# The fourth gate's weights: the low half by a subtraction on the chip in place of an accumulating DMA

## The chip, the cores and the metric

One core of a Trainium2 chip runs the whole program. Its engines are TensorE (matmuls, called PE in the profile, with PEld for its weight loads), VectorE (DVE), ScalarE (ACT), GpSimd (POOL) and SyncE (SP), which here only issues DMAs. Each engine takes its instructions strictly in the order in which they were written, and starts one when the semaphores it waits for are set. The metric is device time in microseconds (us) for one call of the kernel, lower is better.

## The reference

One layer of a hybrid decoder for a prompt of 1024 tokens and 8 single-token samples, which share their weights. What is computed around the change:

```python
h = rmsnorm(x, g_mix)
u = h @ w_in                      # 1024 -> 1536 columns
a    = u[..., :512]               # pooling branch
val  = u[..., 512:1024]
gate = u[..., 1024:]
glu  = val * jax.nn.sigmoid(gate)
yb   = conv_mixer(g_ext, ...)     # causal depthwise conv, 31 taps, on glu
x = x + concat(ya, yb) @ w_out
x = x + cross_attn(rmsnorm(x), k, v) @ w_o
x = x + (silu(h @ w_gate) * (h @ w_up)) @ w_down
```

All arrays are float32, and the result must be of float32 accuracy.

## The kernel before

**Split operands.** The large matmuls of this kernel get their operands as `fp32r`, and for accuracy each operand is held as two such parts, high and low, and a product is made in three passes: high by high, low data by high weights, high data by low weights (`PASSES`). So each block of raw weights, 128 x 1024, has to be turned into a tile `w` of two parts before PE can use it. There are two ways:

- `split`: one pass copies the raw weights into the high part (ACT or POOL, L373 or L375), and one subtraction, raw minus high, makes the low part (DVE or POOL, L384).
- `split_by_dma`: one pass copies the raw weights into the high part (L395 on ACT or L397 on POOL), a second pass writes minus the high part into the low part (the same line), and a DMA issued by POOL (L402) adds the raw weights from HBM onto it (`accum_op=ADD`).

The table `BY_DMA` names, for each weight array, the blocks that go the second way.

```python
        if j in BY_DMA.get(name, ()):
            split_by_dma(lambda p: w[:, p], lambda p: (w, p), lambda: raw[:], 1024, [(raw,)],
                         lambda: io[name][j], [], name not in ("w_dn", "w_dn2"))
        else:
            split(lambda p: w[:, p], lambda p: (w, p), lambda: raw[:], 1024, [(raw,)])
```

**What runs where.** Blocks of `w_in` come in pairs gate, value for the four channel groups (blocks 0 to 7: the gates are 0, 2, 4, 6), then four blocks of the pooling branch. A block gives one group of 72 matmuls on PE, L480, eight steps over the 1024 inputs by three passes by three column chunks of 344 tokens. Behind PE, DVE multiplies the gate's PSUM result by the norm factor (L714), ACT takes the sigmoid (L715), POOL multiplies once more (L716), and DVE multiplies with the value's result into `glu` (L730). The blocks of the pooling branch leave PSUM by L836 on DVE, with a tiny copy of the last 8 columns, L806.

**The convolution** of the 512 channels in four groups fills DVE, ACT and POOL beside PE. Half of its taps are multiply-adds on DVE (L682, L684, accumulating in PSUM, `cacc`). The other half are products on ACT into one of four rotating buffers (L664, `cp`; sometimes POOL, L665) that are added to `y` by POOL or DVE (L667, one after the other, since all add to the same rows; the lengths 511 down to 497 tell which tap a row is). L654 starts such a chain, L692, L693, L696, L697 and L701 end a group, L703 adds its sum to the total.

**Behind it** the memory keys (L850; their PSUM is emptied by L854 on DVE, then split by L373 or L375 and L384 into `kT`), values (L927, L932), windows of the pooling branch (L814 to L828, on POOL or DVE) and its small map (L870) are put on PE before the output projection (L480, `oa`, `ob`), the queries and the scores, and then the feed-forward part (L1323), which takes half of the span.

**What sets the order.** The pieces are named in the table `ORDER` (`g3 v3` is the fourth gate and value). `Program.order` goes through all tasks with modelled costs, and decides at each step which task is written next and, where a task may run on two engines, on which one. A planner's cost therefore decides at build time who makes a tap or a split. Buffers are reused by tags; `w` has two places (so the weights of a group are made while PE works on the group before), `raw` has three. The weights of the fourth gate are block 6 of `w_in`; their tile is `w_871` in the rows below, their raw tile `raw_549`.

Of the kernel before, what the change touches and what calls it, by code (L numbers as in the profile page):

```python
# [46 lines left out]
)  # L47

BY_DMA = {"w_in": (3, 4, 6, 7, 9, 10, 11), "w_k": (2, 3, 5), "w_o": (4, 5, 6), "w_out_a": (1,), "w_out_b": (3,), "w_q": (4, 5, 6), "w_v": (0, 7), "w_dn": (18, 19), "w_dn2": (1,)}
WIDE = ("w_k", "w_v")  # L50
LEAD = {"w_k": 2, "w_v": 3, "w_out_a": 15, "w_q": 15, "w_in": 1, "w_out_b": 12, "w_o": 8}
LAST_SPANS = ((0, 512), (512, 260), (772, 260))
# [208 lines left out]
def hybrid_step_kernel(ctx: ExitStack, tc: tile.TileContext, io):  # L261
# [11 lines left out]
    def buf(name, tag, shape, dtype=F32):  # L273
        return Buf(name, tag, shape, dtype)
# [115 lines left out]
    def split_by_dma(dst, key, src, n, r, again, again_keys, pool_too=False):  # L390


        def scaled(e, p, src, factor):
            if e is nc.scalar:
                e.activation(dst(p), src, AF.Copy, scale=factor)  # L395
            else:
                e.tensor_scalar(dst(p), src, factor, 1.0, ALU.mult, ALU.mult)  # L397

        either = {"ACT": act(n), "Pool": pool_ts(n)} if pool_too else {"ACT": act(n)}
        add(either, lambda e: scaled(e, 0, src(), 1.0), r, [key(0)])  # L400
        add(either, lambda e: scaled(e, 1, f32(dst(0)), -1.0), [key(0)], [key(1)])
        add({"Pool": 0.6}, lambda e: e.dma_start(dst(1), again(), accum_op=ALU.add), [key(1)] + again_keys, [key(1)], nbytes=4 * P * n)  # L402
# [38 lines left out]
    def w_prep():  # L441
# [3 lines left out]
        w = buf(f"w{i}", "op" if name in WIDE or i >= len(seq) - 4 else "w", (P, 2, 1024), F32R)  # L445
        if j in BY_DMA.get(name, ()):
            split_by_dma(lambda p: w[:, p], lambda p: (w, p), lambda: raw[:], 1024, [(raw,)],
# [1399 lines left out]
```

## Time and profile before

| | us |
|---|---|
| median of 3 runs | 1219.01 |
| lowest and highest of them | 1218.43, 1219.83 |
| the profiled execution | 1218.82 |
| its span, first to last instruction | 1217.0 |
| PE busy in it | 1197.5 |
| DVE, ACT, POOL busy | 928.6, 526.1, 246.3 |
| 0 to 35 us | first loads, first gate and value |
| 35 to 148 us | remaining blocks of `w_in`, with the convolution on DVE, ACT and POOL |
| 148 to 215 us | memory keys and values, pooling windows and map, start of the output projection |
| 215 to 545 us | output projection, queries, attention |
| 545 to 1217 us | feed-forward part and final norm |

A row of the profile's groups or of its timeline has the source line, the engine, the operation and the tiles (out<-in, buffer numbers left out). In the timeline the first number is the start, the second how long the row lasted; a bracket gives the idle time of that engine just before, and what ended it. Consecutive instructions of one kind stand as one row with their number (x9).

### The profile page before, as it was taken

Reading aid. Unit: us, or ns where it says so; the run is one execution under the profiler, and the core shown is the slowest. Engines: PE = TensorE matmul, PEld = TensorE weight load, DVE = VectorE, ACT = ScalarE, POOL = GpSimd, SP = SyncE. Lnnn points to the kernel's source line nnn. Section 1 sums busy time; section 2 is a strip of 40 time slices with the busy share of each in tenths; the row PEclk is TensorE's granted clock in tenths of the full one; section 3 lists DMA queues with packets and bytes.
Section 4 is the critical chain, followed back from the end, with each engine's and each line's share of the span. In section 5 each row is a group of like instructions: output and inputs, shape, how many; then the busy total and the mean of one; then the engine's idle time right before and its main releaser. Section 6 shows DMA issues by size and latency. Waiting matters only on the chain.

```text
span 1217.0 us, 19404 instructions
## 1 busy us (share of the span) xinstructions
PE 1197.5 (98%) x7720; PEld 1122.1 (92%) x7720; DVE 928.6 (76%) x1551; ACT 526.1 (43%) x720; POOL 246.3 (20%) x294
## 2 busy tenths in 40 slices
PE   8999999999999999999999999999999999999997
PEld 7999988999999979989999999999999999999886
DVE  7999999766258875779777787777867797879754
ACT  7765656445134633444222322233222365544533
POOL 3568842231111102111000000000000034332101
PEclk9999999999999999999999999999999999999999
DMA  7335677326395773521332232222313598678612
GB/s 289 83 76 114 145 211 222 119 103 212 105 294 181 235 276 111 157 104 62 105 114 79 98 114 107 107 83 98 123 70 105 203 319 242 178 185 226 150 52 88
DMA packets 60586, 180.75 MB, mean 149 GB/s; under 512 B 7824, under 2 KB 11600, under 8 KB 59216
## 3 DMA queue, kind: packets, MB, share of 16 engines
q1 hardware_dynamic: 53824, 157.92, 37.6%
q0 software_dynamic: 6672, 21.60, 10.2%
q8 instruction: 60, 0.98, 0.3%
q14 instruction: 30, 0.25, 0.1%
HBM read 145.72 MB, written 33.78 MB: 147 GB/s over the span
## 4 chain that ended last, share of the span: by engine, by line
PE 80%; DVE 3%; DMA 1%; ACT 0%; issue 0%; DVEq 0%; ACTq 0%
PE pr L1323 49%; PE ps L480 7%; PE po L480 7%; PE fd L1666 6%; PE oa L480 4%; PE ob L480 4%; PE sc L1023 1%; PE vps L927 1%; DMA w<-in_w_q 1%; PE pv L1081 1%; PE kps L850 0%; PE pmap L870 0%; DVE spcache_k L1120 0%; DMA spcache_k<-in_cache_k 0%; DVE oo L1086 0%; DVE pT L1067 0%
## 5 line engine op out<-in xcount | busy, mean ns | idle before, releaser
L1323 PEld LDWEIGHTS pr<-ab,wTb 128*128 128x128 f32 x1056 | 132.1, 188 | 3.6
L1323 PE MATMUL pr<-ab,wTa 128*128 128x260 f32 x1056 | 133.6, 282 | 0.0
L1323 PE MATMUL pr<-ab,wTb 128*128 128x260 f32 x1056 | 133.3, 282 | 0.0
L1323 PEld LDWEIGHTS pr<-ab,wTa 128*128 128x128 f32 x1056 | 130.7, 189 | 2.0 <-DVE su L1339 0.3
L1323 PE MATMUL pr<-ab,wG 128*128 128x512 f32 x528 | 128.8, 393 | 0.0
L1339 DVE TENSOR_TENSOR su<-pr,su 128x520 f32<-128x520 f32 (+1 forms) x112 | 77.7, 695 | 57.4 <-PE pr L1323 57.2
L480 PE MATMUL ps<-xop,w 128*128 128x344 f32 x720 | 114.1, 320 | 0.0
L1323 PEld LDWEIGHTS pr<-ab,wG 128*128 128x128 f32 x528 | 96.3, 188 | 18.8
L480 PEld LDWEIGHTS ps<-xop,w 128*128 128x128 f32 x720 | 113.6, 188 | 0.0
L1323 PEld LDWEIGHTS pr<-hb,dV 128*128 128x128 f32 x768 | 98.7, 188 | 4.4 <-DVE pp L1339 0.3
L1323 PE MATMUL pr<-hb,dV 128*128 128x260 f32 x768 | 100.2, 283 | 0.0
L480 PE MATMUL ps<-xq,w 128*128 128x344 f32 x576 | 94.8, 321 | 0.4 <-DMA w<-in_w_q 0.4
L480 PEld LDWEIGHTS po<-oo,w 128*128 128x128 f32 x576 | 90.9, 188 | 0.6 <-DVE oo L1086 0.4
L480 PEld LDWEIGHTS ps<-xq,w 128*128 128x128 f32 x576 | 90.7, 188 | 0.8 <-DMA w<-in_w_q 0.7
L480 PE MATMUL po<-oo,w 128*128 128x344 f32 x576 | 91.4, 320 | 0.0
L684 DVE SCALAR_TENSOR_TENSOR cacc<-glu,vec,cacc 128x511 f32<-128x511 f32 (+14 forms) x116 | 76.9, 742 | 0.0
L1323 PE MATMUL pr<-hb,dW 128*128 128x512 f32 x288 | 74.4, 394 | 0.0
L373 ACT ACTIVATE w<-raw 128x1024 fp32r<-128x1024 f32 (+1 forms) x37 | 35.0, 951 | 81.7 <-issue 20.1
L1666 PE MATMUL fd<-ho,w 128*128 128x260 f32 (+1 forms) x432 | 69.0, 321 | 0.0
L1666 PEld LDWEIGHTS fd<-ho,w 128*128 128x128 f32 x432 | 62.0, 188 | 6.8 <-issue 0.5
L1350 POOL MEMSET su<- 128x16 f32 x22 | 2.5, 112 | 310.0 <-PE pr L1323 244.0
L1323 PE MATMUL pr<-ab,wU 128*128 128x512 f32 x264 | 64.8, 394 | 0.0
(306 smaller groups left out, 2183.7 us busy)
## 6 DMA issues: line engine op xcount, KB each, us to landing
gr<-in_w_gu SPq DMA_DIRECT2D x44, 512.0 KB, 3.6
hb<-su SPq DMA_DIRECT2D x8, 1040.0 KB, 4.6
hs<-hb SPq DMA_DIRECT2D x16, 520.0 KB, 6.3
dr<-in_w_dn SPq DMA_DIRECT2D x16, 512.0 KB, 3.7
spcache_k<-in_cache_k SPq DMA_DIRECT2D x12, 512.0 KB, 6.3
hs<-hb SPq DMA_DIRECT2D x12, 512.0 KB, 4.7
raw<-in_w_in SPq DMA_DIRECT2D x10, 512.0 KB, 3.8
hb<-he SPq DMA_DIRECT2D x8, 520.0 KB, 3.4
```

Source lines behind the costliest of these rows:

```text
L373: e.activation(dst(0), src(), AF.Copy, scale=1.0 if gain is None else gain)
L480: e.matmul(ps[:, c, :CW], w[:, wi, cols], x[:, xi, c * CW : (c + 1) * CW], start=first and p == 0, stop=last and p == 2)
L684: e.scalar_tensor_tensor(acc[h][:, n:], src[:, : HALF - n], w, acc[h][:, n:], ALU.mult, ALU.add)
L927: e.matmul(ps[:, m], memg[k // 4][:, xi, k % 4, m * P : (m + 1) * P], w[:, wi, col : col + 512], start=(k == 0 and p == 0), stop=(k == KT ...
L1023: e.matmul(bank()[:, i * NMEM : (i + 1) * NMEM], qop[2 * h + dt][:, qi, tt * P : (tt + 1) * P], kk[:, ki, 2 * (h % 2) + dt], start=(dt == ...
L1081: e.matmul(ps[:, c], v[:, vi, m, col : col + P], pT[h][m][:, pi, sl], start=(m == 0 and p == 0), stop=(m == 1 and p == 2))
L1323: e.matmul(bank(c), w[:, wi, cols(j)], xs[0](j, xi)[:, c * n : (c + 1) * n], start=onto is None and j == 0 and p == 0, stop=j == nj - 1 an ...
L1339: from_sums(sums, "DVE", dve, lambda e, src, sl: e.tensor_tensor(as_banks(o(sl), src), src, as_banks(a(sl), src), op), [akey], [okey])
L1350: add({"Pool": 0.12}, lambda e: e.memset(o(), 0.0), [], keys)
L1666: e.matmul(view(i), w[:, wi, col : col + P], hops[k][:, xi, half, lo - half * HALF + i * width // count : lo - half * HALF + (i + 1) * wid ...
```

## The change

The number 6 leaves the list of `w_in` in `BY_DMA`. The fourth gate's weights are then made by `split` and no longer by `split_by_dma`.

```diff
-BY_DMA = {"w_in": (3, 4, 6, 7, 9, 10, 11), "w_k": (2, 3, 5), "w_o": (4, 5, 6), "w_out_a": (1,), "w_out_b": (3,), "w_q": (4, 5, 6), "w_v": (0, 7), "w_dn": (18, 19), "w_dn2": (1,)}
+BY_DMA = {"w_in": (3, 4, 7, 9, 10, 11), "w_k": (2, 3, 5), "w_o": (4, 5, 6), "w_out_a": (1,), "w_out_b": (3,), "w_q": (4, 5, 6), "w_v": (0, 7), "w_dn": (18, 19), "w_dn2": (1,)}
```

The order of the instructions on PE and on SP is the same as before. On ACT, DVE and POOL the planner's order is different from the fourth gate's weights to the start of the output projection, and the same again from there.

On ACT, where the fourth gate's weights are made (`cacc_1_576` is the odd accumulator of the first convolution group, `w_981` and `w_983` the weights of the fourth value):

```order
 L664 ACTIVATE cp<-y_571,csum 128x509
-L395 ACTIVATE w_871<-raw_549 128x1024
-L395 ACTIVATE w_871<-w_871 128x1024
+L373 ACTIVATE w_871<-raw_549 128x1024
+L664 ACTIVATE cp<-y_571,csum 128x508
 L715 ACTIVATE t_873<-t_873 128x1032
-L664 ACTIVATE cp<-y_571,csum 128x508
 L664 ACTIVATE cp<-y_571,csum 128x506
-L664 ACTIVATE cp<-y_571,csum 128x505
 L692 ACTIVATE y_571<-cacc_1_576,vec 128x511
 L693 ACTIVATE y_571<-vec 128x1
+L664 ACTIVATE cp<-y_571,csum 128x505
```

One of the two passes over the weights is gone, and L692, which empties the odd accumulator, has two instructions fewer ahead of it. On POOL at the same place (`t_873` is the third gate's sigmoid, `y_571` holds the convolution sums of the first two groups):

```order
 L667 TENSOR_TENSOR y_571<-y_571,cp 128x497
 L667 TENSOR_TENSOR y_571<-y_571,cp 128x510
+L384 TENSOR_TENSOR w_871<-raw_549,w_871 128x1024
+L716 TENSOR_TENSOR t_873<-t_873,Rx 128x1032
 L667 TENSOR_TENSOR y_571<-y_571,cp 128x509
-L716 TENSOR_TENSOR t_873<-t_873,Rx 128x1032
-L402 DMA w_871<-in_w_in 128x1024
 L667 TENSOR_TENSOR y_571<-y_571,cp 128x508
 L667 TENSOR_TENSOR y_571<-y_571,cp 128x507
 L667 TENSOR_TENSOR y_571<-y_571,cp 128x506
 L667 TENSOR_TENSOR y_571<-y_571,cp 128x505
+L402 DMA w_981<-in_w_in 128x1024
```

The subtraction stands on POOL, ahead of the third gate's product, and the DMA issue behind that product is gone.

On DVE at the end of the third convolution group (its sum is in `y_1098` before, `y_1125` now; the 511 is the first tap of the fourth group), before:

```order
L654 TENSOR_TENSOR y_1098<-glu_985 128x512
L667 TENSOR_TENSOR y_1098<-y_1098,cp 128x501
L684 SCALAR_TENSOR_TENSOR cacc_1_1184<-glu_985,vec,cacc_1_1184 128x499
L684 SCALAR_TENSOR_TENSOR cacc_0_1182<-glu_985,vec,cacc_0_1182 128x498
L684 SCALAR_TENSOR_TENSOR cacc_1_1184<-glu_985,vec,cacc_1_1184 128x498
L684 SCALAR_TENSOR_TENSOR cacc_0_1182<-glu_985,vec,cacc_0_1182 128x497
L667 TENSOR_TENSOR y_1098<-y_1098,cp 128x511
L667 TENSOR_TENSOR y_1098<-y_1098,cp 128x498
L701 TENSOR_TENSOR y_1098<-cacc_0_1182,y_1098 128x512
L836 TENSOR_TENSOR a_1440<-ps_1312,Rx 128x1032
L806 COPY side<-a_1440 128x8
```

And now:

```order
L654 TENSOR_TENSOR y_1125<-glu_984 128x512
L667 TENSOR_TENSOR y_1125<-y_1125,cp 128x501
L667 TENSOR_TENSOR y_1125<-y_1125,cp 128x500
L667 TENSOR_TENSOR y_1125<-y_1125,cp 128x499
L667 TENSOR_TENSOR y_1125<-y_1125,cp 128x498
L667 TENSOR_TENSOR y_1125<-y_1125,cp 128x511
L667 TENSOR_TENSOR y_1125<-y_1125,cp 128x497
L836 TENSOR_TENSOR a_1436<-ps_1313,Rx 128x1032
L696 TENSOR_TENSOR y_1125<-y_1125,cacc_0_1156 128x512
L697 TENSOR_TENSOR y_1125<-y_1125,cacc_1_1169 128x512
L806 COPY side<-a_1436 128x8
```

Three additions of taps (500, 499 and 497) that POOL made are now DVE's, and the six of this place stand in one run behind the multiply-adds.

On POOL around the second memory key block (`kT_1648` before, `kT_1649` now; `w_1701` and `w_1703` are the second half of the third key block's weights), before:

```order
L384 TENSOR_TENSOR kT_1648<-kf_1631,kT_1648 128x512
L814 COPY win_1640<-win_1640 128x2x2
L815 TENSOR_TENSOR win_1640<-win_1640 128x2x510
L384 TENSOR_TENSOR kT_1648<-kf_1703,kT_1648 128x512
L402 DMA w_1701<-in_w_k 128x1024
```

And now:

```order
L384 TENSOR_TENSOR kT_1649<-kf_1636,kT_1649 128x512
L814 COPY win_1641<-win_1641 128x2
L815 TENSOR_TENSOR win_1641<-win_1641 128x2x511
L375 TENSOR_SCALAR kT_1649<-kf_1706 128x512
L384 TENSOR_TENSOR kT_1649<-kf_1706,kT_1649 128x512
L402 DMA w_1703<-in_w_k 128x1024
```

The high part of the second key block, before on ACT, stands on POOL, one instruction more ahead of the DMA issue; POOL and DVE have changed places in two levels of the window sums.

## The prediction

> **What bounds the kernel now.** I read first the page's busy shares, then what PE waited for, then the busy time by stage.
>
> ```profile
> span 1217.0 us, 19404 instructions
> PE 1197.5 (98%) x7720; PEld 1122.1 (92%) x7720; DVE 928.6 (76%) x1551; ACT 526.1 (43%) x720; POOL 246.3 (20%) x294
> ```
>
> PE is busy for 98% of the span. What can be gained or lost shows as waits of PE, and these are few (line, what it waited for: us in total, times, longest):
>
> ```profile
> PE psg L480 <- ACT w L373: 5.2, 1, 5.2
> PE pv L1081 <- DVE oo L1086: 1.8, 2, 1.2
> PE Rf_ps L510 <- DVE xss L411: 1.8, 1, 1.8
> PE pmap L870 <- DVE kf L854: 0.4, 1, 0.4
> PE ps L480 <- DMA w<-in_w_q: 0.4, 1, 0.4
> ```
>
> The 5.2 are the first loads. Between there and the output projection, where the change acts, PE waits once, 0.4 us. By stage:
>
> ```profile
> 80.00:130.00 50.00, 50.00 (x319) 50.00 (x318) 48.02 (x72) 30.70 (x41) 44.05 (x35) 1.00 0.51 117
> 130.00:154.00 24.00, 24.00 (x166) 24.00 (x165) 22.96 (x33) 13.64 (x19) 20.21 (x15) 1.00 0.69 157
> 154.00:179.00 25.00, 24.58 (x152) 21.53 (x151) 24.38 (x45) 12.86 (x16) 11.03 (x13) 1.00 0.85 220
> ```
>
> After the length of a stretch come PE, PEld, DVE, ACT and POOL. PE is full from 80 to 154 us, and DVE nearly so (48.0 of 50, 23.0 of 24, 24.4 of 25). PE leads, DVE follows close behind, and at 178 us they meet:
>
> ```profile
> 176.45 1.90 PE L870 MATMUL pmap<-win,wmap 128*128 128x344 f32 x6
> 178.03 0.69 DVE L854 TENSOR_TENSOR kf<-kps,side 128x512 f32<-128x512 f32 x1
> 178.77 2.00 PE L870 MATMUL pmap<-win,wmap 128*128 128x344 f32 x6 [0.42 <-DVE kf L854]
> ```
>
> PE is ready for this map at 178.35 and waits 0.42 us until DVE has emptied a PSUM place. So the question is how late DVE arrives at its L854 of 178.03, and whether a weight arrives late somewhere.
>
> **The DMA that goes, and what takes its place.** The fourth gate's weights before:
>
> ```profile
> 80.15 1.06 ACT L395 ACTIVATE w<-raw 128x1024 fp32r<-128x1024 f32 x1 [0.61 <-PE ps L480]
> 81.25 1.06 ACT L395 ACTIVATE w<-w 128x1024 fp32r<-128x1024 f32 x1
> 85.72 0.86 POOL L402 DMA_DIRECT2D w<-in_w_in  x1
> DMA to landing us min/median/max: 5.5/5.5/5.5
> 91.51 1.06 ACT L395 ACTIVATE w<-raw 128x1024 fp32r<-128x1024 f32 x1 [0.34 <-PE ps L480]
> ```
>
> The addition landed at 85.72 + 5.5 = 91.2; PE came to this group when the one before ended, 91.5. It was in time, so its end gains PE nothing: term 0. Now the high part is there at 81.2 and POOL subtracts at once:
>
> ```profile
> L384 POOL TENSOR_TENSOR w<-raw,w 128x1024 fp32r<-128x1024 f32 x6 | 14.9, 2549 | 6.7 <-ACT w L373 6.7
> 76.89 1.86 DVE L667 TENSOR_TENSOR y<-y,cp 128x499 f32<-128x499 f32 x3
> ```
>
> The low part is ready at 81.3 + 2.55 = 83.9, 7.6 us before its use. POOL has 2.55 more and the issue of 0.86 less, 1.7 us more work. On POOL that hides: its next fixed point is the following block's DMA issue, which waits for ACT's pass that waits for PE at 91.5. What POOL does not get done goes to DVE: three taps, which take 1.86 in a row like the one shown, so DVE has **+1.9 us** before 178 us.
>
> **What DVE gets back.** Rows of DVE's idle time, and of what ends it:
>
> ```profile
> 83.17 1.92 ACT L664 ACTIVATE cp<-y,csum 128x508 f32<-128x508 f32 x3
> 83.50 0.69 DVE L697 TENSOR_TENSOR y<-y,cacc 128x512 f32<-128x512 f32 x1
> 84.99 0.67 ACT L692 ACTIVATE y<-cacc,vec 128x511 f32<-128x511 f32 x1
> 85.69 0.75 DVE L682 TENSOR_SCALAR cacc<-glu,vec 128x512 f32<-128x512 f32 x1 [1.50 <-ACT y L692]
> 132.71 0.68 DVE L667 TENSOR_TENSOR y<-y,cp 128x501 f32<-128x501 f32 x1 [0.97 <-POOL y L667]
> 150.76 2.41 POOL L384 TENSOR_TENSOR w<-raw,w 128x1024 fp32r<-128x1024 f32 x1 [1.11 <-ACT w L373]
> 151.11 2.09 DVE L806 COPY side<-a 128x8 f32<-128x8 f32 x1
> L806 DVE COPY side<-a x3: 172/514/2091, 127.7 to 151.1; 128x8 f32<-128x8 f32 x3
> ```
>
> First, DVE stood 1.50 us for L692. That now has a pass over the weights (1.06) and a tap (1.92 / 3 = 0.64) less ahead of it: 84.99 - 1.70 = 83.3, and ends at 84.0, when DVE is still at L697 (83.50 to 84.19). The wait is gone: **-1.5 us**. Second, at 132.71 DVE waited 0.97 for a tap of POOL. Now the six taps stand in a run behind the multiply-adds, so some of that wait goes and a shorter one, for ACT's products, may come: I take -0.4, between 0 and -1.0. So by 140 us DVE is 1.9 - 1.5 - 0.4 = 0.0 us later than before, at the ends 1.9 later and 0.6 earlier.
>
> Third, the copy of 8 columns lasts 0.17 us alone but took 2.09 at 151.11, ending with POOL's subtraction that had begun 0.35 before: this copy cannot run beside it. So DVE's clock is set anew at 151.11 + 2.09 = 153.2 by POOL, however late it is up to 2 us. POOL's subtraction in turn waits for loads. Two loads ahead of it change places in the raw buffers: by the built programs' addresses the second key weights no longer take the place that is freed at 115.3, but that of the first key weights, which POOL's subtraction frees at 110.30 + 2.66 = 113.0.
>
> ```profile
> 110.30 2.66 POOL L384 TENSOR_TENSOR w<-raw,w 128x1024 fp32r<-128x1024 f32 x1
> 115.32 0.90 SPq L359 DMA_DIRECT2D raw<-in_w_k  x2
> 119.22 1.06 ACT L373 ACTIVATE w<-raw 128x1024 fp32r<-128x1024 f32 x1 [2.83 <-DMA raw<-in_w_k]
> ```
>
> The load comes 2.3 us earlier, ACT's wait of 2.83 for it should shrink to 0.5, and POOL run up to 2 us ahead until its next issue that depends on PE. What of it is left at 150.76 lies between 0 and 1; I take 0.5. From there the same instructions stand on DVE up to L854, in another order. So L854 comes some 0.5 us earlier, more than PE's wait of 0.42: **-0.4 us**, bounded by 0 and -0.4 from this.
>
> **Sum.** Addition gone 0, POOL's subtraction 0 (hidden behind PE's group from 80 to 91.5), three taps on DVE +1.9, L692 -1.5, tap wait -0.4, reset by the copy, PE's wait at 178.77 -0.4. The profiled execution has 1218.82 with a span of 1217.0, 1.8 outside; its time is 0.2 under the median of 1219.01. So 1218.8 - 0.4 = 1218.4 for such an execution, and 1218.6 us for the median. If none of the covers on DVE held, nor the reset, it would be +1.9: 1220.9. The difference is well under 0.2% (2.4 us), which is about what a measurement of this kernel can tell from no change.
>
> The Trainium skill, "SBUF — State Buffer", section "Who interferes with whom", says that a DVE instruction with two SBUF inputs, or a DVE copy in its two-port mode, and a GpSimd instruction that reads SBUF exclude each other for a whole instruction, whichever came second waiting. The copy of 2.09 agrees with that. It speaks against moving a two-input subtraction onto POOL beside DVE; at 81 to 84 us DVE's rows read PSUM for one input, so by that rule too the term stays 0.
>
> **Rivals.** *POOL is shut out, and a weight lands late (slower).* The row for it, and the margin:
>
> ```profile
> L665 POOL TENSOR_SCALAR cp<-y,csum 128x503 f32<-128x503 f32 x1 | 6.2, 6217 | 15.8 <-DVE y L667 15.8
> L665 POOL TENSOR_SCALAR cp<-y,csum 128x511 f32<-128x511 f32 x1 | 1.0, 1003 | 0.0
> 163.29 3.30 DVE L684 SCALAR_TENSOR_TENSOR cacc<-glu,vec,cacc 128x499 f32<-128x499 f32 x5
> 164.89 1.30 POOL L384 TENSOR_TENSOR kT<-kf,kT 128x512 fp32r<-128x512 f32 x1
> 166.58 1.20 DVE L815 TENSOR_TENSOR win<-win 128x1016 f32<-128x1016 f32 x1
> 168.93 0.27 DVE L827 TENSOR_REDUCE win<-side 128x8 f32<-128x128 f32 x1
> L402 POOL DMA_DIRECT2D w<-in_w_k x1: 876/876/876, 166.1 to 166.1; - x1
> DMA to landing us min/median/max: 6.0/6.0/6.0
> 170.71 5.90 PE L850 MATMUL kps<-memg,w 128*128 128x256 f32 x48
> ```
>
> A product of some 500 elements that lasts 1.0 us elsewhere lasted 6.2 on POOL, while DVE ran tensor-tensor rows without a break. Now POOL makes the high and the low part of the second key block behind L854, and DVE goes into such a run (L815, L384, L815) three multiply-adds behind L854, 3 x 3.30 / 5 = 2.0 us. If POOL's L384 is not begun by then, it stands until L827, and the DMA issue of 166.1 comes at about 170.2. Its weights, here at 172.1 now, are needed at 170.71 + 2.95 = 173.7 and would land at 176.2: PE stands 2.5 us, or 2.9 if DVE's delay adds to the map's wait: 1221.9. For it: the row of 6.2 us. Against: POOL needs 1.0 us for the high part and has 2.0, so its L384 begins 1 us ahead of the run. Chance 0.17.
>
> *DVE becomes the bound.* The waits it gives back turn up again as others, and the reset at 151 does not catch it: three taps 1.9, and one more copy held by a whole subtraction, 2.4, with nothing recovered, would be 4.3 us late at L854, 1223.3. Against: the reset swallows up to 2.1 of it, which leaves 2.2, 1221.2. Only the part beyond that decides. Chance 0.11 that it passes 0.2%.
>
> *The gaps further on close (faster).* To be faster by 0.2% PE would have to lose 2.4 us of waits, and near the change it has 0.4. It would need the ones at L1081 and L510 as well (1.8 each), 0.4 + 1.8 + 1.8 = 4.0 at most, 1215.0. PE's and DVE's orders there are unchanged, so I see nothing that would close them. Chance 0.09.
>
> **How the numbers follow.** No measurable change 0.63, around 1218.6, its own range 1217.4 to 1220.9 (the unabsorbed taps); POOL shut out 0.17; DVE 0.11; gaps 0.09. Faster by over 0.2% is the last, 0.09; within 0.2% 0.63; slower the two others, 0.28. The range reaches upward into the slower cases and leaves the faster one out: 1216.9 to 1222.6.
>
> **What would show it.** In the changed profile: no wait of DVE for L692 near 85 us; POOL's L384 of about 2.5 us from 81.3; the second key weights loaded by SP near 113 and ACT's wait at 119 down to about 0.5; the copy near 151 ending with POOL's subtraction; PE without a gap at this stage, or 0.4 at the map. I am wrong if PE shows a wait for a DMA at the third key block or at the output projection, if L854 comes later than 179, or if the time moves by over 2.4 us with no wait of PE between 80 and 215 us.

## The result, and the profile after

The changed kernel takes 1222.77 us (median of 13 runs, 1221.08 to 1226.46); the kernel before, timed beside it, 1219.71 us (1218.43 to 1221.03). The ratio is 1.0024, with a 95% interval of 1.0013 to 1.0034: slower by some 3 us. The forecast was no measurable change, 1218.6 us; the measured time lies just above its range of 1216.9 to 1222.6. Its base was the 1219.01 of three runs, and the kernel before came out 0.7 us above that here; with the base that much higher the same range would have held the time. What failed is the forecast of no change: the change itself, 3.1 us, is above the 2.4 us within which the prediction saw none, and two of its signs of being wrong are there: a wait for a DMA at the third key block, and an L854 later than 179 us.

The page of the profiled execution of the changed kernel (1221.56 us):

```profile
span 1219.7 us, 19406 instructions
PE 1197.9 (98%) x7720; PEld 1121.1 (92%) x7720; DVE 931.2 (76%) x1553; ACT 526.0 (43%) x719; POOL 243.8 (20%) x292
```

The span has grown by 2.7 us, and PE's busy time by 0.4 only. So PE stands more. What it waited for (line, cause: us in total, times, longest), without the rows that are as before:

```profile
PE pmap L870 <- DVE kf L854: 1.6, 1, 1.6
PE psg L480 <- DVE xop L386: 0.8, 1, 0.8
PE ss L1133 <- DVE spcache_k L1120: 0.6, 1, 0.6
PE kps L850 <- DMA w<-in_w_k: 0.6, 1, 0.6
```

The wait for L854 was 0.4, the one for a key weight was not there. The other two lie outside the part that changed: the 0.8 (0.3 before) at the start, the 0.6 at 367 us. Their size goes up and down in the runs below (L1133 had 1.4, 0.2 or nothing), and I did not follow them.

By stage (after the length come PE, PEld, DVE, ACT, POOL), the last row for the 50 us in which the loss lies; there PE had 49.48 before:

```profile
80.00:130.00 50.00, 50.00 (x319) 50.00 (x318) 48.75 (x70) 30.11 (x40) 44.52 (x34) 1.00 0.48 108
130.00:154.00 24.00, 24.00 (x166) 24.00 (x165) 23.58 (x36) 14.48 (x20) 16.27 (x13) 1.00 0.55 118
154.00:179.00 25.00, 24.42 (x151) 21.45 (x149) 24.63 (x44) 12.55 (x14) 12.82 (x13) 1.00 0.94 252
150.00:200.00 50.00, 47.73 (x269) 40.09 (x269) 48.87 (x78) 26.82 (x29) 19.77 (x17) 1.00 0.71 192
```

PE is full up to 154 us in both kernels. DVE is fuller than before in all of the first three stretches: 48.75 for 48.02, 23.58 for 22.96, 24.63 for 24.38, 1.6 us in all. A held instruction counts as busy in these rows. And where the loss shows, in the timeline:

```profile
165.52 0.62 POOL L375 TENSOR_SCALAR kT<-kf 128x512 fp32r<-128x512 f32 x1 [0.95 <-DVE kf L854]
167.46 0.89 POOL L402 DMA_DIRECT2D w<-in_w_k  x1
174.81 2.89 PE L850 MATMUL kps<-memg,w 128*128 128x256 f32 x22 [0.57 <-DMA w<-in_w_k]
177.54 1.90 PE L870 MATMUL pmap<-win,wmap 128*128 128x344 f32 x6
180.23 0.69 DVE L854 TENSOR_TENSOR kf<-kps,side 128x512 f32<-128x512 f32 x1
181.06 1.97 PE L870 MATMUL pmap<-win,wmap 128*128 128x344 f32 x6 [1.62 <-DVE kf L854]
```

L854 comes at 180.23 in place of 178.03: DVE is 2.20 us late, and PE is held up by it at the second map. That is 1.2 us more of waiting there, and 0.6 for the weight, of the 2.7; the rest of this execution's difference lies outside the part that changed and is not explained here. The weight is late through the same lateness: POOL waits 0.95 for DVE's L854 of the second key block (164.74 for 162.69 before), and its DMA issue behind that is at 167.46 for 166.13.

**Where DVE lost the time.** The place where it got something back, at 85 us, timeline of POOL, ACT and DVE:

```profile
81.34 2.42 POOL L384 TENSOR_TENSOR w<-raw,w 128x1024 fp32r<-128x1024 f32 x1 [0.26 <-ACT w L373]
84.28 0.69 ACT L692 ACTIVATE y<-cacc,vec 128x511 f32<-128x511 f32 x1 [0.84 <-DVE y L697]
85.00 0.76 DVE L682 TENSOR_SCALAR cacc<-glu,vec 128x512 f32<-128x512 f32 x1 [0.76 <-ACT y L692]
```

The subtraction runs when and as long as expected. But L692 was not free to start at 83.3: it waits 0.84 until DVE's L697 has ended, which reads the same accumulator. DVE's L682 comes 0.69 earlier than before, not 1.5.

Then the place where it lost most, and this I had not priced. In the timeline of the kernel before, POOL and DVE near 128 us:

```profile
125.44 2.25 POOL L667 TENSOR_TENSOR y<-y,cp 128x506 f32<-128x506 f32 x2
127.76 1.29 POOL L667 TENSOR_TENSOR y<-y,cp 128x504 f32<-128x504 f32 x1
127.69 0.17 DVE L806 COPY side<-a 128x8 f32<-128x8 f32 x1
128.99 0.88 POOL L402 DMA_DIRECT2D w<-in_w_in  x1
```

And in the changed kernel:

```profile
128.30 2.02 DVE L806 COPY side<-a 128x8 f32<-128x8 f32 x1
130.24 2.02 DVE L684 SCALAR_TENSOR_TENSOR cacc<-glu,vec,cacc 128x500 f32<-128x500 f32 x3
128.10 0.88 POOL L402 DMA_DIRECT2D w<-in_w_in  x1 [0.93 <-ACT w L395]
128.71 1.57 POOL L667 TENSOR_TENSOR y<-y,cp 128x504 f32<-128x504 f32 x1
```

A copy of 8 columns takes 2.02 us. It begins 0.2 us into a DMA issue of POOL and ends with the tap behind that issue (130.32 and 130.28). Before, the same copy came in the moment between two taps, 127.69 to 127.76, and took 0.17. DVE stands 1.85 us longer.

What hangs on it, in order of time (line and engine stand in each row):

```profile
134.74 0.68 DVE L654 TENSOR_TENSOR y<-glu 128x512 f32<-128x512 f32 x1
135.46 0.82 ACT L659 ACTIVATE y<-y,vec,csum 128x512 f32<-128x512 f32 x1 [1.93 <-DVE y L654]
139.47 1.22 DVE L836 TENSOR_TENSOR a<-ps,Rx 128x1032 f32<-128x1032 f32 x1
142.60 1.06 ACT L395 ACTIVATE w<-w 128x1024 fp32r<-128x1024 f32 x1
143.57 0.74 DVE L682 TENSOR_SCALAR cacc<-glu,vec 128x512 f32<-128x512 f32 x1
144.01 0.87 POOL L402 DMA_DIRECT2D w<-in_w_k  x1
152.73 2.41 POOL L384 TENSOR_TENSOR w<-raw,w 128x1024 fp32r<-128x1024 f32 x1 [0.79 <-ACT w L373]
153.86 1.30 DVE L806 COPY side<-a 128x8 f32<-128x8 f32 x1
158.98 0.68 DVE L854 TENSOR_TENSOR kf<-kps,side 128x512 f32<-128x512 f32 x1
```

ACT waits 1.93 for DVE's L654, its products and the pass over the key weights come later, POOL's DMA issue for them is at 144.01 (141.69 before), its subtraction at 152.73 (150.76 before). The last copy ends at 155.16, with that subtraction. In the kernel before it ended at 153.20, also with it. The instant that the prediction took for a fixed point has moved by the 2 us that it was to swallow. And DVE itself comes to this copy 2.75 us late (153.86 for 151.11). It has lost this by L682, where the same work lies behind it on DVE in both kernels; before:

```profile
140.80 1.40 DVE L682 TENSOR_SCALAR cacc<-glu,vec 128x512 f32<-128x512 f32 x2
```

143.57 for 140.80 is 2.77 late. The copy near 128 us makes 1.85 of it, the next copy, near 142 us, 0.56 (1.07 us for 0.51), and 0.4 is left for the three taps less what DVE got back. (At L836 it is only 1.66, 139.47 for 137.81, because L701, 0.68 us, stood ahead of L836 before and stands behind it now.)

### The profile page after: what moved, and what is told of

Same layout as the page of the kernel before. It is cut to its first block, busy times and chain, and to the rows that moved or that the text cites. A ratio compares the mean times of both kernels' runs of the same rounds, so it can differ in the third digit from the quotient of the medians.

```text
span 1219.7 us, 19406 instructions
## 1 busy us (share of the span) xinstructions
PE 1197.9 (98%) x7720; PEld 1121.1 (92%) x7720; DVE 931.2 (76%) x1553; ACT 526.0 (43%) x719; POOL 243.8 (20%) x292
## 4 chain that ended last, share of the span: by engine, by line
PE 78%; DVE 4%; DMA 1%; issue 1%; ACT 1%; POOL 0%; DVEq 0%; SPq 0%; ACTq 0%
PE pr L1323 49%; PE po L480 7%; PE fd L1666 6%; PE ps L480 5%; PE oa L480 4%; PE ob L480 4%; PE sc L1023 1%; DVE spcache_k L1120 1%; PE vps L927 1%; PE pv L1081 1%; DMA sbcache_v<-pd 1%; PE kps L850 0%; PE pmap L870 0%; DMA spcache_k<-in_cache_k 0%; DMA pd<-prow 0%
```

## The experiments

All but one keep an order fixed: the planner's list of tasks and engines, taken from the kernel before or from the changed one, stands in the kernel as a table, and the edit is made in the table or in one operation. "Order of before" and "order of after" mean these tables. The ratios are to the kernel before, timed beside each. The copy is the L806 near 128 us.

| run | what | copy us | L854 at | PE waits at the map for L854 / for a key weight | ratio, 95% interval |
|---|---|---|---|---|---|
| before | | 0.17 | 178.03 | 0.4 / 0 | 1 |
| after | | 2.02 | 180.23 | 1.6 / 0.6 | 1.0024 (1.0013 to 1.0034) |
| e1 | order of before, subtraction | 1.02 | 177.82 | 0 / 0 | 1.0005 (0.9997 to 1.0014) |
| e2 | order of after, DMA addition | 1.91 | 180.66 | 2.4 / 0 | 1.0024 (1.0013 to 1.0034) |
| e3 | after, copies as sums | 0.16 | 177.49 | 0 / 0 | 0.9994 (0.9982 to 1.0005) |
| e7 | after, one copy as a sum | 0.16 | 178.45 | 0.7 / 0 | 1.0007 (0.9996 to 1.0019) |
| e10 | after, the copy at another place | 0.18 | 178.85 | 1.1 / 0 | 1.0006 (0.9993 to 1.0019) |
| e8 | before, taps on DVE | 1.26 | 179.19 | 1.7 / 0 | 1.0018 (1.0008 to 1.0028) |
| e9 | before, copy later | 0.63 | 178.59 | 0.7 / 0 | 0.9998 (0.9990 to 1.0007) |
| e6 | after, taps on POOL | 2.04 | 180.87 | 0.4 / 2.7 | 1.0043 (1.0030 to 1.0056) |

The copy, L854 and the waits are those of the one profiled execution of each run, the ratio is that of all its executions. The profiled one of e6, 1221.51 us, is the fastest of its six, so its waits show less than e6 loses. Stamps of two executions can be compared to about 0.2 us: PE's first L850 of the first key block starts at 147.97 to 148.34 in these profiles.

**The operation or the order (e1, e2).** Instructions in POOL's order; e1 against before (without ACT's negating pass and POOL's DMA issue for these weights), e2 against after (there ACT negates again, right behind the high part):

```diff
 L667 TENSOR_TENSOR y,cp 128x497
 L667 TENSOR_TENSOR y,cp 128x510
+L384 TENSOR_TENSOR w<-raw,w        (e1)
...
-L384 TENSOR_TENSOR w<-raw,w        (e2)
+L402 DMA w<-in_w_in                (e2)
```

> The order of the kernel before, pinned as a table, with the one operation exchanged in it: ACT's negating pass and the DMA addition of the fourth gate's weights are gone, POOL subtracts 2.4 us at 81 us. Nothing else changes its place or its engine. Before is 1219.7, the change 1222.8. Theory 1 (the reordered plan costs the time: three taps on DVE and a copy L806 that falls beside POOL's work at 128 us): 1219.0 to 1220.2, PE's wait at the pmap of 179 us stays under 0.6 us. Rival (the subtraction itself costs it, by keeping POOL 1.7 us longer or by contending with DVE): 1222.3 to 1223.3, PE's waits of 1.6 and 0.6 us turn up here too.

> The order of the changed kernel, pinned, with the old operation put back in it: ACT negates right behind the high part, and POOL issues the DMA addition where its subtraction stood. The three taps stay on DVE and every other instruction at the changed kernel's place. Theory 1 (the plan costs it): 1222.3 to 1223.3, the copy L806 near 128 us lasts about 2 us, PE waits 1.2 to 1.8 us at the pmap. Rival (the operation): back at 1219.2 to 1220.2.

e1 came out at 1220.09 us and e2 at 1222.30, against 1219.8 for before. In e1 the subtraction stands in the same place as in the changed kernel, also from 81.34 for 2.42 us, and PE has no wait at all for L854. In e2, with the DMA addition back, PE waits longer than in the changed kernel:

```profile
PE pmap L870 <- DVE kf L854: 2.4, 1, 2.4
```

So the operation costs nothing that can be measured, and the order that the planner makes around it costs the whole. Theory 1 holds in both by the time. The waits of e2 are not quite those expected: 2.4 at the map for 1.2 to 1.8, and none for the weight.

**The copy (e3, e7, e10, e4).** The same eight columns by another instruction; in e7 only for the copy near 128 us, in e4 in the order of before:

```diff
-add({"DVE": 0.07}, lambda e: e.tensor_copy(st_pool()[:, g, :, 15], ab[:, ai, SEQ:T]), ...
+add({"DVE": 0.07}, lambda e: e.tensor_reduce(st_pool()[:, g, :, 15],
+        ab[:, ai, SEQ:T].unsqueeze(2), axis=AX.X, op=ALU.add), ...
```

> The changed kernel in its own order; only the copy L806 of 8 columns is written as a sum over an axis of one element, so that it moves the same numbers by another form of DVE instruction. Theory 1 with the copy as its deciding part: the instruction near 128 us lasts 0.2 to 0.3 us in place of 2.03, those at 142 and 154 us lose 0.7 and 1.1, DVE comes 2 us earlier to L854, PE's waits of 1.6 and 0.6 us go: 1219.8 to 1221.0. Rival (the three taps alone, or the late weight of the third key block, whatever the copy does): 1222.3 to 1223.3. If the form is held up just as the copy is, it lasts 2 us again and the time stays at 1222.8.

> The changed kernel in its own order, only the copy L806 of the third window group, the one near 128 us that lasted 2.03 us, as a sum over one element; those near 142 and 154 us stay copies. If that one copy decides: DVE is 1.9 us earlier from 130 us, the copy near 151 us swallows what the taps cost (it ends with POOL's subtraction at 153 as before), PE's wait at the pmap is under 0.6: 1219.2 to 1220.6. If the later copies decide (0.9 and 1.1 us above their bare time in the changed kernel): 1221.5 to 1222.8.

e3 took 1218.98 us, 0.8 below the range expected, and e7 1220.12. In e3 all four instructions run in 0.16 to 0.17 us (count, then shortest, median and longest in ns):

```profile
L806 DVE TENSOR_REDUCE side<-a x4: 160/166/168, 46.7 to 151.2; 128x8 f32<-128x8 f32 x4
151.25 0.17 DVE L806 TENSOR_REDUCE side<-a 128x8 f32<-128x8 f32 x1
```

The second row is the last of them: with the three taps on DVE and nothing held, DVE comes to it 0.14 after the 151.11 of the kernel before.

In e7, with one instruction's form changed, the timeline of DVE, and one row of POOL and ACT:

```profile
128.28 0.88 POOL L402 DMA_DIRECT2D w<-in_w_in  x1 [0.93 <-ACT w L395]
128.45 0.16 DVE L806 TENSOR_REDUCE side<-a 128x8 f32<-128x8 f32 x1
133.75 0.82 ACT L659 ACTIVATE y<-y,vec,csum 128x512 f32<-128x512 f32 x1
137.76 1.23 DVE L836 TENSOR_TENSOR a<-ps,Rx 128x1032 f32<-128x1032 f32 x1
152.17 1.23 DVE L806 COPY side<-a 128x8 f32<-128x8 f32 x1
178.45 0.68 DVE L854 TENSOR_TENSOR kf<-kps,side 128x512 f32<-128x512 f32 x1
```

It stands in the same 0.2 us of the same DMA issue and isn't held. ACT's wait of 1.93 is gone. L836 comes at 137.76; before it came here:

```profile
137.81 1.22 DVE L836 TENSOR_TENSOR a<-ps,Rx 128x1032 f32<-128x1032 f32 x1
```

That is the same within the 0.2 us of the stamps, but L701 stands behind L836 now. At L682, with the same work left, DVE is 1.07 late (141.87 for 140.80), of which 0.55 is the second copy, 1.06 us for 0.51. So the three taps, less what DVE got back, are worth some 0.5 us, and at the end of the last copy (152.17 + 1.23 = 153.40 for 153.20) DVE is 0.2 behind. What is left of e7's ratio is within its interval; its other copies are still held, 1.06 and 1.23 us, and L854 is 0.4 late.

e10 leaves the copy's form and moves it:

```diff
 L836 TENSOR_TENSOR a<-ps,Rx 128x1032
 L684 SCALAR_TENSOR_TENSOR cacc<-glu,vec,cacc 128x501
-L806 COPY side<-a 128x8
...
 L654 TENSOR_TENSOR y<-glu 128x512
+L806 COPY side<-a 128x8
```

> The changed kernel; the copy L806 of 128.3 us keeps its form and goes behind L654 on DVE, to about 133 us, where POOL's row of taps has ended (POOL has nothing from 132.8 to 139.1). If POOL's running instruction is what holds the copy, it lasts 0.17 us there, and the time is that of the run with this one copy as a sum (1220.1): 1219.2 to 1220.8. If the copy form is slow here for another reason: 2 us again and 1222.3 to 1223.3.

1219.81 us. The copy at a place where POOL rests, in DVE's timeline:

```profile
133.57 0.18 DVE L806 COPY side<-a 128x8 f32<-128x8 f32 x1
```

Form and place lead to the same end, so what holds the copy is POOL's running work. The Trainium skill, "SBUF — State Buffer", section "Who interferes with whom", says that a DVE copy in its two-port mode and a GpSimd instruction shut each other out, and that on trn2 a `tensor_reduce` never contends: e3, e7 and e10 agree (0.16 beside POOL's work, 0.18 in its rest), though no row says which mode the copy runs in. It also says that whichever is issued first has the ports. For the DMA issue, from 128.10, that fits. Between the copy and the tap the trace does not bear it out: by their stamps the copy stood from 128.30, the tap began at 128.71, and the tap went first.

> The kernel before in its own order, with only the form of the copy L806 changed, as in the changed kernel with the sum over one element (which came out at 1219.0). The copy at 151.1 us, 2.09 us before, lasts 0.2. If that copy kept DVE back on the path that sets the end, L854 comes up to 1.9 us earlier and PE's last wait of 0.4 us at the pmap goes: 1219.2 to 1219.6. If it was hidden (DVE waits elsewhere instead): 1219.6 to 1220.0. Both views say that no more than 0.5 us is to be had here, against 3.8 us in the changed order: what the copy costs hangs on how late DVE already is.

e4: 1219.02 us, ratio 1.0000 (0.9990 to 1.0010), a little under both ranges. In the order of before the same edit gains nothing that can be measured, although a copy of 2.09 us goes. PE waited only 0.42 us for DVE there, so more was not to be had; which of the two views is right this run does not tell.

**The taps (e5, e6, e8), and the copy without them (e9).** In e8 and e9 the order of before, in e5 and e6 that of after. e5 has POOL's row as in e6, but there the three taps stand ahead of the products that they add, so that what they add is stale:

```diff
e6, POOL, and the same three off DVE; e8 the other way round:
 L667 TENSOR_TENSOR y<-y,cp 128x502
+L667 TENSOR_TENSOR y<-y,cp 128x500
+L667 TENSOR_TENSOR y<-y,cp 128x499
+L667 TENSOR_TENSOR y<-y,cp 128x497
 L667 TENSOR_TENSOR y<-y,cp 128x510
e9, DVE:
-L806 COPY side<-a 128x8
 L684 SCALAR_TENSOR_TENSOR cacc<-glu,vec,cacc 128x501
 L684 SCALAR_TENSOR_TENSOR cacc<-glu,vec,cacc 128x501
+L806 COPY side<-a 128x8
```

> The changed kernel in its own order, but the three taps of the third conv group that had moved to DVE (500, 499, 497 columns) stand on POOL again, behind the others there as before. Theory 1 (DVE's extra work decides): DVE is 1.9 us less late at L854, PE's wait at the pmap falls from 1.6 to 0.4 or less: 1220.8 to 1221.8. Rival (POOL has no room for them: 3 times about 1.6 us there push its DMA issues for the following blocks and the tap chain that DVE waits for): 1222.8 or more, with a wait of DVE for a tap of POOL of over 1 us near 133 us. By the third view (the copy held at 128 us decides and the taps do not) 1222.3 to 1223.3, with the copy at 2 us.

> The changed kernel in its own order, the three taps (500, 499, 497 columns) at their places in the program but on POOL, so that each comes behind the product it adds (in the earlier run with the taps on POOL they stood ahead of their products, and what was added was stale). If the three taps on DVE are a needed part of the lateness: PE's wait at the pmap falls from 1.6 to 0.4 or less, 1220.0 to 1221.5. If POOL has no room for them, as the earlier run's 1223.5 suggests: 1222.8 to 1224.0, since POOL's DMA issue for the fifth to eighth key weights and the taps that DVE adds to come later.

> The order of the kernel before, with its DMA addition, and only the three taps (500, 499, 497 columns) moved from POOL to DVE at the places where they stand in the program. DVE has 3 times 0.64 = 1.9 us more work at 131 to 138 us, POOL 3 times some 1.3 us less; the copy at 127.7 us lies ahead of them and stays at 0.2 us. If the copy near 151 us swallows up to 2 us of delay, as the prediction had it: 1219.4 to 1220.3. If the taps alone make the loss: 1221.5 to 1222.8, with PE's wait at the pmap at 1.5 us or more.

> The order of the kernel before; only the copy L806 near 127.7 us stands two multiply-adds (1.3 us) later on DVE, about where the changed kernel has it against POOL's DMA issue and tap. It should be held, for 1 to 2 us. If lateness of DVE is what costs, the copy alone is absorbed: the wait of 0.97 us for POOL's tap at 132.7 shrinks, the copy near 151 us swallows the rest: 1219.0 to 1220.2, PE's wait at the pmap 0.7 or less. If one held copy is enough by itself: 1221 to 1222.8.

e5 took 1223.48 us (ratio 1.0036, 1.0019 to 1.0052), e6 1224.26. So POOL has no room for the taps: in e6 DVE waits 2.78 us for one of them. PE's wait for L854 does fall to 0.4 there, the figure of the first view, but not because DVE is earlier (L854 is at 180.87): PE itself comes late, by a weight:

```profile
176.69 2.89 PE L850 MATMUL kps<-memg,w 128*128 128x256 f32 x22 [2.69 <-DMA w<-in_w_k]
```

That the planner gave the taps to DVE was right, then. e8 took 1220.91 us, between its two ranges, with a wait of 1.7 as the second had it, but it did not isolate the taps: the copy near 128 us, which the edit does not touch, was held in this run.

```profile
127.54 1.26 DVE L806 COPY side<-a 128x8 f32<-128x8 f32 x1
128.72 0.73 DVE L684 SCALAR_TENSOR_TENSOR cacc<-glu,vec,cacc 128x501 f32<-128x501 f32 x1
126.33 2.44 POOL L667 TENSOR_TENSOR y<-y,cp 128x505 f32<-128x505 f32 x2
```

DVE arrived 0.15 us earlier than in the kernel before and met a tap that ran to 128.77. Taps and held copy together cost 1.0018 here too. The taps with this copy free are e3, e7 and e10: no loss that the intervals show. The held copy without the taps on DVE is e1 (1.02 us) and e9 (0.63, less than was meant): none either. In e1 the 0.97 that DVE waited for POOL's tap at 132.71 is gone, and L682 is only 0.2 late (141.00 for 140.80): the held copy went into that wait. In e9 the wait stays at 1.0, against its expectation, and L682 is 0.6 late. In e7, with the taps on DVE and this copy free, the wait is gone as well, so the taps leave no room for a held copy. As far as these runs go it takes both. In e5 and e6 the copy is held for 2.05 and 2.04 without the taps on DVE, but there the taps load POOL; a copy held for the full 2 us with nothing else added was not among the runs.

**What carried the lateness on (e12), and telling the planner (e11).** e12 puts one tap that POOL makes ahead of its weights' passes behind them again, as before. In this run that tap adds what then stands in its product's buffer, which has been filled anew.

```diff
 L667 TENSOR_TENSOR y<-y,cp 128x509
-L667 TENSOR_TENSOR y<-y,cp 128x508
 L397 TENSOR_SCALAR w<-raw 128x1024
...
 L384 TENSOR_TENSOR w<-raw,w 128x1024
+L667 TENSOR_TENSOR y<-y,cp 128x508
 L667 TENSOR_TENSOR y<-y,cp 128x507
```

> The changed kernel; on POOL the tap of 508 columns of the third group stands again behind the weights' passes and subtractions of 141 to 155 us, as before, and not ahead of them. POOL reaches L397 at 141.7 in place of 143.0 and its last subtraction of that run 1.3 us earlier, at 151.4, and the copy at 142 us (1.07) is held less. If the copies behind POOL's work are what carries the lateness on to L854, that is up to 1.3 us of it: PE's wait at the pmap 0.4 to 1.0 in place of 1.6, 1221.0 to 1222.0. If DVE's own work carries it: 1222.3 to 1223.3.

1222.94 us, ratio 1.0032 (1.0021 to 1.0044): a miss for the first view, that POOL's own work made its subtraction late. POOL does reach L397 at 141.53, but then it stands for ACT, and the subtraction and the copy come as late as in the changed kernel (POOL, then DVE):

```profile
143.84 0.89 POOL L402 DMA_DIRECT2D w<-in_w_k  x1 [1.26 <-ACT w L395]
153.41 1.94 DVE L806 COPY side<-a 128x8 f32<-128x8 f32 x1
```

So POOL's subtraction is late through ACT's pass, behind the products that wait for DVE's L654. DVE itself comes to the copy 2.30 late (153.41 for 151.11). The last edit is one argument:

```diff
-    [ak, (side, "pool")], [(side, "pool", g)])
+    [ak, (side, "pool")], [(side, "pool", g)], lock=True)
```

> The changed kernel, with the planner told that L806 excludes POOL's work (lock=True, as it has for the tensor-tensor instructions); the planner then makes a new order from the first window group on, with other taps on DVE and POOL. Its copies should each last under 1 us. If the plan's blindness to this copy is the root: 1218.5 to 1220.5. A new plan may have misses of its own, which can't be worked out ahead: up to 1223.

1230.24 us, ratio 1.0079 (1.0063 to 1.0096), the slowest of all and above both expectations. The copies near 131 and 139 us take 0.17 and 0.18, but the new plan has other misses (PE's waits):

```profile
PE ob L480 <- DVE opb L384: 3.6, 2, 2.0
PE kps L850 <- DMA w<-in_w_k: 3.1, 1, 3.1
```

No run is shown to be faster than the kernel before. e3 has the lowest ratio, and its interval holds 1; against the changed kernel, whose interval begins at 1.0013, it is faster.

## Why the prediction was wrong

- **The addition's end, 0, and POOL's subtraction, 0:** right. e1 has the subtraction in the old order at no measurable cost, e2 the addition in the new order at no gain.
- **Three taps on DVE, +1.9:** nearly right in size; 4.21 us for the six in a row is 0.70 each, 2.1 for the three. e6 shows what they would cost on POOL.
- **The wait for L692, -1.5:** mis-sized, -0.7. The step counted what stands ahead of L692 on ACT and overlooked that L692 would have to wait for DVE's L697, although it named that row.
- **The tap wait at 132.71, -0.4:** it went altogether, -0.97. The three terms as measured make 2.1 - 0.7 - 0.97 = 0.4 at L682, the forecast was 0.0, and e7, where the copy near 128 us is free, has 0.5 without the hold of the second: up to there the sum was right within half a microsecond, by luck in part, since the errors of the terms partly cancel.
- **The copy, the step that failed.** The prediction showed the row "172/514/2091" and its sum has a hold only for the copy that was already held. The other two were left at the durations they had, a term of 0 without a reason, although the same argument had just moved DVE and POOL against each other. The first of them went from 0.17 to 2.02, the second from 0.51 to 1.07: 2.4 us of the 2.77 by which DVE is late at L682.
- **The reset at 153.2:** right only while nothing that POOL waits for hangs on DVE. In e7 the copy ends at 153.40, as forecast. In the changed kernel L654 was late enough for ACT to wait 1.93 for it, and POOL's subtraction moved with DVE; besides, DVE came 2.75 late, more than it could swallow. The prediction followed the subtraction back to loads and stopped there.
- **The swap of the loads:** right. ACT's pass over the second key weights runs at 116.34 without a wait, 2.9 us earlier, and POOL is 0.9 ahead at the DMA issue that the copy met (128.10 for 128.99). DVE gained nothing by it.
- **L854 0.5 earlier, PE -0.4:** wrong as what precedes it: 2.2 later, +1.2 and a late weight of 0.6.

What happened was the second rival, "DVE becomes the bound", in its own terms: the taps and one more copy held by POOL, 2.2 us left at L854. It was given 0.11, against the reset, and its 1221.2 was the lower end of what it gave. The first rival's late weight turned up too, but not by the mechanism that it named alone. In the changed kernel (0.6) POOL's subtraction is not shut out, it lasts 1.30 as before; it starts late, behind the L854 that DVE brings late. In e6 (2.7) POOL comes to it 2.3 us late (167.15 for 164.89, 166.22 in the changed kernel), and the subtraction is then held for 0.9 more (2.22 for 1.30).

## What to carry to other kernels

A short instruction that another engine can shut out has no duration of its own: when a change moves two such engines against each other, every one of them is priced from its bare time to the length of what may be running beside it (here from 0.17 to over 2 us), not only the one that was held before. A fixed point is fixed only if its whole chain of waits, back through every engine, does not come round to the engine that is late. And when a planner makes the order, hold the order and exchange the operation, then the reverse; here these two runs settled in one step that the operation was free.

## What was unexpected

A copy of 8 columns on DVE waited for two instructions of POOL, a DMA issue and the tap behind it, 2.02 us, where a sum over one element at the same place ran in 0.16. During the first 0.4 us of that wait POOL ran nothing but the DMA issue.

The profiled execution of e4, 1223.99 us, is 5.0 us longer than e4's median, and its profile shows a loss at the start (PE's wait, then DVE and POOL):

```profile
PE Rx_ps L510 <- DVE Rx_m L512: 3.5, 1, 3.5
32.77 3.36 DVE L384 TENSOR_TENSOR w<-raw,w 128x1024 fp32r<-128x1024 f32 x1
32.66 2.39 POOL L384 TENSOR_TENSOR w<-raw,w 128x1024 fp32r<-128x1024 f32 x1
```

DVE's and POOL's subtractions came at the same moment, DVE's took 3.36 in place of 1.22 and ended 1.1 us behind POOL's, and L512 behind it kept PE for 3.5.
